# w_down's operands over other buffers of w_up, two sums of w_up in the preparation tiles, and the second half's first left parts behind the result copies

## The chip, the cores and the metric

The kernel runs on one core of one Trainium2 chip. A core has a matmul engine (TensorE, PE in the profile, with its weight loads as PEld), three engines for elementwise work (VectorE or DVE, ScalarE or ACT, GpSimd or POOL), a queue that issues most of the DMAs (SyncE, SP), an on-chip memory for tiles and eight banks in which matmuls accumulate. Each engine works through its own instructions in their order and waits on semaphores for the others. The metric is the device time of one execution in microseconds.

## What is computed

One encoder layer on 2048 tokens of width 1024, in float32: a norm, one wide product, a windowed and a neighbourhood attention, gates, a projection, and then the part that matters here, the feed-forward block:

```python
x = x + merged @ w_out[l]
h2 = rms_norm(x, norm_mlp[l])
x = x + jnp.square(jax.nn.relu(h2 @ w_up[l])) @ w_down[l]      # 1024 -> 4096 -> 1024
return rms_norm(x, norm_final)
```

## The kernel before

All products in float32 are made of three matmuls: each operand is split into a rounded half (a cast on ACT, line 277) and the rest (a subtraction on DVE, line 278), and lines 281, 282 and 283 multiply high by high, high by low and low by high. A left operand (the weights in w_up, the activations in w_down) is loaded into PE, a right one streams through it. A matmul of 128 x 128 by 128 x 512 is the unit.

**w_up** multiplies in two halves of the tokens (m = 0, 1), each in eight quads (q) of the 4096 features. A quad is one step of a seven-product scheme (Strassen's, in Winograd's form): products n = 1, 5, 6, 2, 7, 4, 3, each for two blocks a of 128 features, 12 matmuls a block, 24 a product, 168 a quad. Six of the eight banks serve a quad: x for n = 1 and 2, y for 6, 7 and 4, z for 5 and 3. What leaves a bank:

- n = 1: ACT copies x into a tile c1 (line 1497), and only then may n = 2 go on in x.
- n = 6: DVE adds y and c1 into u2, and only then may n = 7 go on in y.
- n = 2: relu and square on ACT give the block c11. n = 7, 4, 3: more sums on DVE (line 272), relu (1457) and square (1460) on ACT.
- After n = 3, DVE makes four more sums of the finished blocks (s1, a21, s2, s4), the left operands of w_down. All seven are stored to DRAM (`keep`, line 1479; tensor `at`), with tiles from the ring `c`, 11 tiles.

The left parts of a quad come from `up_left_steps`: the quad's weights lie in two tiles `uraw`, sums of them in `uS`, the seven split operands in the rings `uwhla` (one buffer) and `uwhlb` (two buffers), taken in turn. A cast into one of the three buffers has to wait for the product that read it three parts earlier. The right parts of a half lie in seven pairs of pages, `ubh1` to `ubh7`. The ring `chunk`, four tiles, serves for preparing the second half's right parts during the first half's quads 1 to 6 (`ahead`, `parts_ahead`) and is idle otherwise.

**w_down** is again one step of the seven-product scheme, now over the whole matrix. For each product n and each of 16 slices k it loads the stored block into `da` (512 KB) and the weights into `dw` (256 KB), splits them into `dah` and `dwh` (four buffers each), and runs 24 matmuls, three for each of eight banks (t = 0 to 7). The buffers of w_down are laid into the memory that w_up leaves, in the order in which the rings are made; a first write to such a buffer waits for the last reader of what lay there. Before, `dah` lies over `ubh1` and `uwhlb`, and `dwh` over `uwhla` and a part of `uraw`.

What sets the order: the program is written as a sequence, and a scheduler with its own model of times orders each engine's instructions. Marks such as `issue_after(x)` keep an instruction from being placed ahead of x; they make no wait on the chip.

Of the kernel before, what the change touches and what calls it, by code (L numbers as in the profile page):

```python
# [8 lines left out]
F32 = mybir.dt.float32  # L9
F32R = mybir.dt.float32r  # L10
# [12 lines left out]
P = 128  # L23
KC = D // P
NB = 4
BT = 512
# [66 lines left out]
def encoder_layer(ctx, tc, x, norm_mix, w_in, b_gate, sink, rpb, w_pa, w_pb, w_out,  # L93
                  norm_mlp, w_up, w_down, norm_final, dist_a, mask_b, out):
    nc = tc.nc
    V, A, G, PE, SY = nc.vector, nc.scalar, nc.gpsimd, nc.tensor, nc.sync

    def pool(name, side=None, space=None, stack=None):
        kw = {"reuse_waits": "tile"} if space is not DRAM else {}
        if side:  # L100
            kw["side"] = side
        if space:
            kw["space"] = space
        return (stack or ctx).enter_context(tc.tile_pool(name=name, bufs=1, **kw))
# [19 lines left out]
    def T(pl, shape, dt, tag, bufs):  # L124
        n_t[0] += 1
        pl = pl[tag] if isinstance(pl, dict) else pl
        return pl.tile(shape, dt, tag=tag, bufs=bufs, name=f"{tag}_{n_t[0]}")
# [131 lines left out]
    def by_token(c):  # L259

        return c.rearrange("p (t a c) -> p t a c", t=4, a=4)

    def by_place(c):

        return c.rearrange("p (a t c) -> p t a c", t=4, a=4)
# [10 lines left out]
    def split(src, hi, lo, eng):  # L276
        rounded[0] = A.copy(hi, src).ins  # L277
        return eng.tensor_tensor(out=lo, in0=src, in1=hi.bitcast(F32), op=ALU.subtract).ins  # L278
# [10 lines left out]
    def ring(stack, tag, shape, dt, bufs, side="right"):  # L289

        pl = pool(f"r_{tag}", side=side, stack=stack)
        return lambda: T(pl, shape, dt, tag, bufs)
# [17 lines left out]
    def zbank(pl, bufs=1):  # L310
        n_ps[0] += 1
        return pl.tile([P, 512], F32, tag="b", bufs=bufs, name=f"zb_{n_ps[0]}")
# [265 lines left out]
    right = {n: (in_page[n](), in_page[n]()) for n in (1, 2)}  # L578
    tbanks = [(tpool, 2), (zpool[0], 1), (tpool, 2), (zpool[1], 1), (ypool[0], 1), (ypool[1], 1)]
    for k in range(KC):  # L580
        ps = zbank(*tbanks[k % 6])
# [21 lines left out]
    for p in range(2):  # L603
        t = T(xp, [P, D], F32, "xin", 8).rearrange("p (k c) -> p k c", k=4)
        c = QUADS[2][0]
# [14 lines left out]
    for k in range(KC):  # L620
        ps = zbank(*tbanks[k % 6])
# [135 lines left out]
    for q in range(2, len(QUADS)):  # L757
# [15 lines left out]
        if q == SECOND:  # L773
            right, b0 = right2, 2
# [5 lines left out]
        lf = list(in_left(ws, QUADS[q][1], (1, 2) if q == 2 else (), ORDER if q == 2 else ORDER_3))  # L780
# [485 lines left out]
    up_page, up_rings = {}, {}  # L1266
# [14 lines left out]
    def up_whl():  # L1281
        n_whl[0] += 1
        return (up_rings["whla"] if n_whl[0] % 3 == 1 else up_rings["whlb"])()

    def up_weights(q, behind=None):
        ws = []
        for p in range(2):
            w = up_rings["raw"]()
            with tc.issue_after(behind) if behind else nullcontext():
                SY.dma_start(w, w_up[0][p * BT : (p + 1) * BT, q * BT : (q + 1) * BT].rearrange("(k p) f -> p k f", p=P))  # L1290
            ws.append(w)
        return ws

    def up_left(ws, behind=None):

        out = {}
        for _ in up_left_steps(ws, out, behind):
            pass
        return out

    def up_left_steps(ws, out, behind=None, eng=V):

        a11, a21 = ws[0][:, :, 0:256], ws[0][:, :, 256:512]
        a12, a22 = ws[1][:, :, 0:256], ws[1][:, :, 256:512]

        def parts(src, eng):
            hl = up_whl()
            split(src, hl[:, 0], hl[:, 1], eng)
            return hl

        with tc.issue_after(behind) if behind else nullcontext():
            out[1] = parts(a11, V)
        yield
        s1 = up_rings["S"]()
        with tc.issue_after(behind) if behind else nullcontext():
            add(V, s1, a21, a22)
        out[5] = parts(s1, V)
        yield
        add(eng, a21, a11, a21, ALU.subtract)
        s2 = up_rings["S"]()  # L1320
        add(eng, s2, a22, a21, ALU.subtract)
        out[6] = parts(s2, eng)
        yield
        out[2] = parts(a12, eng)
        yield
        out[7] = parts(a21, eng)
        yield
        out[4] = parts(a22, eng)
        last_left[0] = rounded[0]
        yield  # L1330
        add(eng, a12, a12, s2, ALU.subtract)
        out[3] = parts(a12, eng)
# [134 lines left out]
            yield  # L1467
        next(rights, None)

    def up_quad(m, q, lf, right, spread):  # L1470

        x, y, z = [None] * 2, [None] * 2, [None] * 2
        c1, u2, c11, c22 = [None] * 2, [None] * 2, [None] * 2, [None] * 2

        def plus(out, ps, c):
            return add(V, by_token(out), by_place(ps), by_token(c))

        def keep(n, a, c):
            stored[0] = SY.dma_start(ats[n][2 * q + a][:, m], c).ins

        for n in (1, 5, 6, 2, 7, 4, 3):
            hl, (rh, rl) = lf[n], right[n]
            last = None
            for a in range(2):
                if n == 1:
                    x[a] = bank()
                elif n == 5:
                    z[a] = bank()
                elif n == 6:
                    y[a] = bank()  # L1490
                ps = {1: x, 2: x, 5: z, 3: z, 6: y, 7: y, 4: y}[n][a]
                at = slice(a * P, (a + 1) * P)
                for k in range(4):
                    mm3s(ps, hl[:, 0, k, at], hl[:, 1, k, at], rh[:, k], rl[:, k], k == 0 and n in (1, 5, 6), k == 3)
                if n == 1:
                    c1[a] = up_rings["c"]()
                    A.copy(by_token(c1[a]), by_place(ps))  # L1497
                elif n == 6:
                    u2[a] = up_rings["c"]()
                    last = plus(u2[a], ps, c1[a])  # L1500
                elif n == 2:
                    c11[a] = up_rings["c"]()
                    squared(c11[a], ps)
                    keep(1, a, c11[a])
                elif n == 7:
                    c22[a] = up_rings["c"]()
                    plus(c22[a], ps, c1[a])
                    last = plus(c22[a], z[a], c22[a])
                    squared(c22[a])
                    keep(4, a, c22[a])  # L1510
                elif n == 4:
                    last = plus(c1[a], ps, c1[a])
                    squared(c1[a])
                    keep(2, a, c1[a])
                elif n == 3:
                    a11, a12, a21, a22 = c11[a], c1[a], u2[a], c22[a]
                    last = plus(a21, ps, a21)
                    squared(a21)
                    s1, s2, s4 = up_rings["c"](), up_rings["c"](), up_rings["c"]()
                    add(V, s1, a21, a22)  # L1520
                    keep(5, a, s1)
                    add(V, a21, a11, a21, ALU.subtract)
                    keep(7, a, a21)
                    add(V, s2, s1, a11, ALU.subtract)
                    keep(6, a, s2)
                    add(V, s4, a12, s2, ALU.subtract)
                    keep(3, a, s4)
            if last:
                with tc.issue_after(last):
                    next(spread, None)  # L1530
# [176 lines left out]
    rights, lf, rest = started  # L1707
    for _ in range(2):
        right = next(rights)
# [7 lines left out]
    for m in range(2):  # L1717
        if m:
            right = next(rights)
            lf = up_left(up_weights(0))  # L1720
        next(rights, None)
        ws = None
        for q in range(8):
            lf = up_left(ws, page_done[0] if m == 0 and q == 1 else None) if q else lf
            if m == 0 and q == 6:
                rights = up_right(1)
                next(rights)
            spread = last_page(rights) if m == 0 and q == 0 else iter(())
            if m == 0 and 1 <= q < 7:
                spread = ahead(q - 2) if 2 <= q < 6 else parts_ahead(1 if q == 1 else 5)  # L1730
            next(spread, None)
            if q < 7:
                ws = up_weights(q + 1, last_dma[0] if m == 0 and q == 0 else None)
            up_quad(m, q, lf, right, spread)
    s_up.close()


    s_dn = ctx.enter_context(ExitStack())
    dw = ring(s_dn, "dw", [P, BT], F32, 8)
    da = ring(s_dn, "da", [P, 2, BT], F32, 4)  # L1740
    dwh = ring(s_dn, "dwh", [P, 2, BT], F32R, 4)
    dah = ring(s_dn, "dah", [P, 2, 2, BT], F32R, 4)
    dt = ring(s_dn, "dt", [P, BT], F32, 2)
    t2_ = ring(s_dn, "t2", [P, BT], F32, 16)
    x2_ = ring(s_dn, "x2", [P, BT], F32, 8)
    p5_ = ring(s_dn, "p5", [P, BT], F32, 8)
    junk_ = ring(s_dn, "junk", [P, BT], F32, 2)
# [20 lines left out]
    t2 = [None] * 16  # L1768
# [89 lines left out]
    for n in (1, 6, 2, 7, 5, 3, 4):  # L1858
        for group in ((range(8),) if n != 4 else (range(4), range(4, 8))):
# [9 lines left out]
            for k in range(16):  # L1869
                lf, rt = left(n, k, part), right_(n, k)  # L1870
# [52 lines left out]
```

## Time and profile before

| | |
|---|---|
| three runs | 2592.23, 2597.12, 2599.40 us (median 2597.12) |
| the profiled execution | 2594.54 us, span of its instructions 2592.8 us |
| w_up, first half | about 1387 to 1666 us of the span |
| w_up, second half | about 1666 to 1972 us |
| w_down | about 1974 us to the end |
| granted matmul clock, mean | 0.997 |

All times in the rows are us from the span's start, each from one profiled execution. A timeline row has the start, the duration, engine, source line, operation, output and inputs with their buffer numbers left out, a count of merged instructions, and in brackets how long the engine had been idle before and what ended it. A row of grouped instructions has busy us and mean ns of one behind the bar. A row of windows has, after the stretch, its length and the busy time of PE, PEld, DVE, ACT and POOL, each with a count, then the granted clock, the DMA engines' busy share and GB/s. A row of the waits has engine and line that waited, whom for, the total in us, how often, and the longest.

### The profile page before, as it was taken

How to read it: one execution, taken by the hardware profiler on the slowest of the kernel's cores; microseconds unless marked ns; L12 is line 12 of the kernel's file. 1: busy time of each engine (PE TensorE's matmuls, PEld its weight loads, DVE VectorE, ACT ScalarE, POOL GpSimd, SP SyncE). 2: the span in 40 equal slices, each digit the busy share in tenths (PEclk: the TensorE clock that was granted, in tenths of full speed). 3: DMA queues.
4: the chain of work that ended last, by engine and by line, in shares of the span. 5: the costliest groups of instructions: out<-in, count | busy, mean ns of one | idle time of the engine just before them, and what ended most of it. 6: DMA issues, size and time to landing. Idle time of an engine off the chain costs nothing.

```text
span 2592.8 us, 34576 instructions
## 1 busy us (share of the span) xinstructions
PE 2541.9 (98%) x11936; PEld 2115.2 (82%) x11936; DVE 1695.4 (65%) x2693; ACT 1311.0 (51%) x2345; POOL 411.9 (16%) x506
## 2 busy tenths in 40 slices
PE   7999999999999999999999999999999999999998
PEld 6788888887887988888887888888887888888887
DVE  8866676667674577646597767866665535554766
ACT  6365464556775676524356555644444322323444
POOL 1000101133345765130312000000000000000011
PEclk9999999999999999999999999999999999999999
DMA  5768868774457899688888666744438835444564
GB/s 187 219 197 249 286 219 275 238 226 112 112 140 190 215 292 264 212 302 304 299 314 257 230 210 224 272 168 164 148 112 297 295 102 186 143 155 157 185 202 162
DMA packets 347999, 552.39 MB, mean 213 GB/s; under 512 B 32120, under 2 KB 152424, under 8 KB 345776
## 3 DMA queue, kind: packets, MB, share of 16 engines
q1 hardware_dynamic: 330640, 509.66, 61.7%
q10 hardware_dynamic: 10944, 24.12, 2.5%
q0 software_dynamic: 6240, 16.40, 2.1%
q8 instruction: 94, 1.54, 0.2%
q14 instruction: 81, 0.66, 0.1%
HBM read 363.35 MB, written 186.71 MB: 212 GB/s over the span
## 4 chain that ended last, share of the span: by engine, by line
PE 84%; DMA 5%; DVE 5%; ACT 2%; issue 1%; SPq 1%; POOL 0%; POOLq 0%; DVEq 0%; ACTq 0%
PE b L282 16%; PE b L283 16%; PE b L281 16%; PE zb L283 5%; PE zb L281 5%; PE zb L282 5%; PE mm L202 3%; PE mm L204 3%; PE mm L203 3%; PE av L1137 2%; PE pt L1157 2%; PE s L1111 1%; PE pt L893 1%; PE b L202 1%; PE b L204 1%
## 5 line engine op out<-in xcount | busy, mean ns | idle before, releaser
L282 PE MATMUL b<-dwh,dah 128*128 128x512 f32 x896 | 348.7, 389 | 0.4 <-DVE dwh L278 0.4
L283 PE MATMUL b<-dwh,dah 128*128 128x512 f32 x896 | 347.7, 389 | 0.0
L281 PE MATMUL b<-dwh,dah 128*128 128x512 f32 x896 | 338.5, 389 | 1.7 <-ACT dwh L277 1.7
L277 ACT CAST dah<-da 128x1024 fp32r<-128x1024 f32 (+1 forms) x128 | 120.8, 946 | 368.6 <-PE b L283 245.8
L281 PE MATMUL zb<-zh,zwhl 128*128 128x512 f32 x728 | 284.6, 391 | 4.0 <-ACT zc L488 1.4
L282 PE MATMUL zb<-zh,zwhl 128*128 128x512 f32 x728 | 284.6, 391 | 0.0
L283 PE MATMUL zb<-zh,zwhl 128*128 128x512 f32 x728 | 283.4, 391 | 1.2 <-DVE zwhl L278 1.2
L278 DVE TENSOR_TENSOR dah<-da,dah 128x1024 fp32r<-128x1024 f32 (+1 forms) x128 | 139.3, 1090 | 213.0 <-ACT dah L277 209.9
L282 PE MATMUL b<-ubh,uwhlb 128*128 128x512 f32 x592 | 231.5, 391 | 3.7 <-DVE ubh L278 3.7
L281 PE MATMUL b<-ubh,uwhlb 128*128 128x512 f32 x592 | 230.7, 390 | 2.3 <-ACT uc L1497 1.6
L283 PE MATMUL b<-ubh,uwhlb 128*128 128x512 f32 x592 | 229.8, 390 | 0.0
L281 PEld LDWEIGHTS b<-dwh,dah 128*128 128x128 f32 x896 | 168.1, 188 | 37.0 <-ACT dwh L277 2.1
L282 PEld LDWEIGHTS b<-dwh,dah 128*128 128x128 f32 x896 | 168.2, 188 | 35.7 <-DVE dwh L278 0.8
L283 PEld LDWEIGHTS b<-dwh,dah 128*128 128x128 f32 x896 | 168.2, 188 | 34.9
L272 DVE TENSOR_TENSOR uc<-b,uc 128x512 f32<-128x512 f32 x160 | 108.9, 689 | 112.8 <-PE b L283 106.9
L281 PEld LDWEIGHTS zb<-zh,zwhl 128*128 128x128 f32 x728 | 136.8, 188 | 34.3 <-ACT zc L488 2.5
L283 PEld LDWEIGHTS zb<-zh,zwhl 128*128 128x128 f32 x728 | 136.7, 188 | 30.0 <-DVE zwhl L278 2.2
L282 PEld LDWEIGHTS zb<-zh,zwhl 128*128 128x128 f32 x728 | 136.7, 188 | 27.9
L202 PE MATMUL mm<-zh,whl 128*128 128x512 f32 x368 | 154.6, 420 | 1.7 <-DVE z L1015 0.9
L204 PE MATMUL mm<-zh,whl 128*128 128x512 f32 x368 | 144.7, 393 | 0.0
L203 PE MATMUL mm<-zh,whl 128*128 128x512 f32 x368 | 144.4, 392 | 0.0
L282 PEld LDWEIGHTS b<-ubh,uwhlb 128*128 128x128 f32 x592 | 111.5, 188 | 27.8 <-DVE ubh L278 4.8
(268 smaller groups left out, 5726.8 us busy)
## 6 DMA issues: line engine op xcount, KB each, us to landing
at<-uc SPq DMA_DIRECT2D x224, 256.0 KB, 2.0
da<-at SPq DMA_DIRECT2D x96, 512.0 KB, 5.0
dw<-in_w_down_dram SPq DMA_DIRECT2D x160, 256.0 KB, 3.7
uraw<-in_w_up_dram SPq DMA_DIRECT2D x32, 1024.0 KB, 13.2
pgl<-wo_d SPq DMA_DIRECT2D x28, 1024.0 KB, 6.3
zraw<-in_w_in_dram SPq DMA_DIRECT2D x24, 1024.0 KB
z<-zg SPq DMA_DIRECT2D x64, 256.0 KB, 5.4
qs_a<-ze SPq DMA_DIRECT2D x32, 256.0 KB, 5.8
```

What stands on the lines that cost most here:

```text
L202: PE.matmul(ps, lh, rh, start=first, stop=False)
L203: PE.matmul(ps, lh, rl, start=False, stop=False)
L204: PE.matmul(ps, ll, rh, start=False, stop=last)
L272: return eng.tensor_tensor(out=out, in0=a, in1=b, op=op).ins
L277: rounded[0] = A.copy(hi, src).ins
L278: return eng.tensor_tensor(out=lo, in0=src, in1=hi.bitcast(F32), op=ALU.subtract).ins
L281: PE.matmul(ps, lh, rh, start=first, stop=False, skip_group_check=True)
L282: PE.matmul(ps, lh, rl, start=False, stop=False, skip_group_check=True)
L283: PE.matmul(ps, ll, rh, start=False, stop=last, skip_group_check=True)
L893: last = PE.transpose(pt[:, h * P : (h + 1) * P], s[:, h, c * P : (c + 1) * P], ident).ins
L1137: PE.matmul(po[0][:, i0 * P : (i0 + ni) * P], v[:kp, c, :], src[:kp, o : o + ni * P], start=first[0], stop=(c == 7 and z == 1), skip_group ...
L1157: last = PE.transpose(pt[:kp, at + (i - i0) * P : at + (i - i0 + 1) * P], s[i][:, rr : rr + kp], ident)
```

## The change

There are three edits. First, the rings of w_down are made in another order: `t2` comes before `dah`, and `dah` before `dwh`. `dah` now lies over `ubh5` and `ubh1`, `dwh` over `ubh6` and `uS`, and `t2` over the buffers of the left parts. Second, in the second half of w_up (and in quad 7 of the first), s1 and s2 take their tiles from `chunk` instead of `c`. Third, at the start of the second half only three of the seven left parts of quad 0 are written ahead of the quad; the four others stand in the quad behind the copies of n = 1.

```diff
-    def up_quad(m, q, lf, right, spread):
+    def up_quad(m, q, lf, right, spread, rest=()):
...
                 if n == 1:
                     c1[a] = up_rings["c"]()
-                    A.copy(by_token(c1[a]), by_place(ps))
+                    copied = A.copy(by_token(c1[a]), by_place(ps)).ins
...
-                    s1, s2, s4 = up_rings["c"](), up_rings["c"](), up_rings["c"]()
+                    of = "chunk" if m or q == 7 else "c"
+                    s1, s2, s4 = up_rings[of](), up_rings[of](), up_rings["c"]()
...
+            for _ in range(5 if rest and n == 1 else 0):
+                with tc.issue_after(copied):
+                    next(rest, None)
...
         if m:
             right = next(rights)
-            lf = up_left(up_weights(0))
+            lf = {}
+            rest = up_left_steps(up_weights(0), lf)
+            for _ in range(3):
+                next(rest)
...
-            up_quad(m, q, lf, right, spread)
+            up_quad(m, q, lf, right, spread, rest if m == 1 and q == 0 else ())
...
+    t2_ = ring(s_dn, "t2", [P, BT], F32, 16)
+    dah = ring(s_dn, "dah", [P, 2, 2, BT], F32R, 4)
     dwh = ring(s_dn, "dwh", [P, 2, BT], F32R, 4)
-    dah = ring(s_dn, "dah", [P, 2, 2, BT], F32R, 4)
     dt = ring(s_dn, "dt", [P, BT], F32, 2)
-    t2_ = ring(s_dn, "t2", [P, BT], F32, 16)
```

The number of instructions on each engine stays the same. Up to the last quad of the first half no engine's order changes.

ACT at the start of w_up's second half. `uwhla` and `uwhlb` are the left parts of quad 0, here those of n = 2, 7 and 4; the two COPY rows are n = 1's copies. Before:

```order
L1460 ACTIVATE uc_15778<-uc_15778 128x512
L277 CAST uwhlb_15981<-uraw_15965 128x1024
L1460 ACTIVATE uc_15793<-uc_15793 128x512
L277 CAST uwhla_15984<-uraw_15963 128x1024
L277 CAST uwhlb_15987<-uraw_15965 128x1024
L1497 COPY uc_16051<-b_16038 128x512
L1497 COPY uc_16066<-b_16053 128x512
L1459 ACTIVATE uc_16136<-b_16038 128x512
```

After the change:

```order
L1460 ACTIVATE uc_15778<-uc_15778 128x512
L1460 ACTIVATE uc_15793<-uc_15793 128x512
L1497 COPY uc_16038<-b_16025 128x512
L1497 COPY uc_16053<-b_16040 128x512
L277 CAST uwhlb_16055<-uraw_15965 128x1024
L277 CAST uwhla_16058<-uraw_15963 128x1024
L277 CAST uwhlb_16061<-uraw_15965 128x1024
L1459 ACTIVATE uc_16136<-b_16025 128x512
```

The two copies stand ahead of the three casts; before, they stood behind them.

DVE at the same place, after the change. `b_16094` and `b_16109` are the two banks of n = 6; the L278 rows are the second halves of the left parts of n = 2, 7 and 4:

```order
L272 TENSOR_TENSOR uchunk_15937<-uchunk_15936,uc_15823 128x512
L272 TENSOR_TENSOR uc_15938<-uc_15737,uchunk_15937 128x512
L272 TENSOR_TENSOR uc_16107<-b_16094,uc_16038 128x512
L272 TENSOR_TENSOR uc_16122<-b_16109,uc_16053 128x512
L278 TENSOR_TENSOR uwhlb_16055<-uraw_15965,uwhlb_16055 128x1024
L278 TENSOR_TENSOR uwhla_16058<-uraw_15963,uwhla_16058 128x1024
L272 TENSOR_TENSOR uraw_15965<-uraw_15965,uS_15976 128x4x256
L278 TENSOR_TENSOR uwhlb_16061<-uraw_15965,uwhlb_16061 128x1024
L272 TENSOR_TENSOR uS_16285<-uraw_16023,uraw_16021 128x1024
```

Before, these three L278 rows, the uraw difference and the uS stood among the sums of quad 7, ahead of the two sums that empty n = 6. PE takes n = 2 (banks `b_16025`, `b_16040`) and the beginning of n = 7 so, after the change:

```order
L283 MATMUL b_16109<-ubh_1843_15957,uwhlb_15978 128x512
L281 MATMUL b_16025<-ubh_1853_15987,uwhlb_16055 128x512
L282 MATMUL b_16025<-ubh_1854_15988,uwhlb_16055 128x512
L281 MATMUL b_16040<-ubh_1853_15987,uwhlb_16055 128x512
L282 MATMUL b_16040<-ubh_1854_15988,uwhlb_16055 128x512
L281 MATMUL b_16094<-ubh_1856_15995,uwhla_16058 128x512
L282 MATMUL b_16094<-ubh_1857_15996,uwhla_16058 128x512
L281 MATMUL b_16109<-ubh_1856_15995,uwhla_16058 128x512
L282 MATMUL b_16109<-ubh_1857_15996,uwhla_16058 128x512
L283 MATMUL b_16025<-ubh_1853_15987,uwhlb_16055 128x512
```

Eight matmuls that need only the cast halves come ahead of the first that needs a DVE half (the last row); before, L281, L282 and L283 of n = 2 alternated from its start.

ACT at the start of w_down. `uc` rows are the last quad of w_up, `dah` and `dwh` the first slices k = 0 to 3. Before:

```order
L1460 ACTIVATE uc_17930<-uc_17930 128x512
L277 CAST dah_18258<-da_18257 128x1024
L277 CAST dah_18292<-da_18291 128x1024
L277 CAST dah_18326<-da_18325 128x1024
L277 CAST dah_18360<-da_18359 128x1024
L1457 ACTIVATE uc_17945<-uc_17945 128x512
L1457 ACTIVATE uc_17986<-uc_17986 128x512
L277 CAST dwh_18262<-dw_18263 128x512
L277 CAST dwh_18296<-dw_18297 128x512
```

After the change:

```order
L277 CAST dah_18258<-da_18257 128x1024
L277 CAST dwh_18262<-dw_18263 128x512
L1457 ACTIVATE uc_18065<-uc_18065 128x512
L1460 ACTIVATE uc_18065<-uc_18065 128x512
L277 CAST dah_18292<-da_18291 128x1024
L277 CAST dwh_18296<-dw_18297 128x512
L1457 ACTIVATE uc_17930<-uc_17930 128x512
L277 CAST dah_18326<-da_18325 128x1024
L1460 ACTIVATE uc_17930<-uc_17930 128x512
L277 CAST dwh_18330<-dw_18331 128x512
L277 CAST dah_18360<-da_18359 128x1024
L277 CAST dwh_18364<-dw_18365 128x512
```

The pairs of a slice stand together, and begin ahead of relu and square of two blocks. DVE follows in the same manner, after the change (`b_17988` is the second bank of y, `b_17947` and `b_17960` are the banks of z):

```order
L278 TENSOR_TENSOR dah_18258<-da_18257,dah_18258 128x1024
L278 TENSOR_TENSOR dwh_18262<-dw_18263,dwh_18262 128x512
L272 TENSOR_TENSOR uc_17930<-b_17973,uc_17930 128x512
L278 TENSOR_TENSOR dah_18292<-da_18291,dah_18292 128x1024
L278 TENSOR_TENSOR dwh_18296<-dw_18297,dwh_18296 128x512
L278 TENSOR_TENSOR dah_18326<-da_18325,dah_18326 128x1024
L278 TENSOR_TENSOR dwh_18330<-dw_18331,dwh_18330 128x512
L272 TENSOR_TENSOR uc_17945<-b_17988,uc_17945 128x512
L272 TENSOR_TENSOR uc_17986<-b_17947,uc_17986 128x512
L278 TENSOR_TENSOR dah_18360<-da_18359,dah_18360 128x1024
L278 TENSOR_TENSOR dwh_18364<-dw_18365,dwh_18364 128x512
L272 TENSOR_TENSOR uc_18001<-b_17960,uc_18001 128x512
```

The sums that empty the last banks now stand between the splits of the pairs; before, three of these four stood ahead of all of them and the last one behind the first two. On PE, the first product of w_down takes L281, L282 and L283 of a bank together; before, the eight L281 of slice 0 came first. The bank after `b_17947` is written by its 15th matmul, the one after `b_17960` by its 26th.

## The prediction

> **What bounds the kernel now.** I read the page's first part, then the table of waits for the matmul engine from 1390 us to the end, then two stages.
>
> ```profile
> PE 2541.9 (98%) x11936; PEld 2115.2 (82%) x11936; DVE 1695.4 (65%) x2693; ACT 1311.0 (51%) x2345; POOL 411.9 (16%) x506
> ...
> PE b L281 <- ACT dwh L277: 1.7, 1, 1.7
> PE b L281 <- ACT uc L1497: 1.6, 1, 1.6
> PE b L282 <- DVE dwh L278: 0.4, 1, 0.4
> ...
> 1700.00:1956.00 256.00, 256.00 (x1131) 211.99 (x1130) 162.32 (x193) 117.28 (x165) 0.00 (x0) 1.00 0.38 134
> 1990.00:2580.00 590.00, 590.00 (x2604) 488.55 (x2603) 334.85 (x462) 211.81 (x328) 10.88 (x12) 1.00 0.55 183
> ```
>
> The matmul engine (PE) sets the end: 98% of the span. In the part that the change reaches, it waits three times, 3.7 us in all: at the start of w_up's second half (L1497) and at the start of w_down (the two dwh rows). Between and behind these places it never pauses; 256.00 us for 1131 matmuls is 0.2263 us each. So what the other engines gain or lose there is worth nothing unless it reaches PE.
>
> **First place: the start of w_up's second half.** PE's and ScalarE's (ACT's) timelines:
>
> ```profile
> 1681.92 0.39 PE L283 MATMUL b<-ubh,uwhlb 128*128 128x512 f32 x1
> 1683.93 0.50 PE L281 MATMUL b<-ubh,uwhlb 128*128 128x512 f32 x1 [1.62 <-ACT uc L1497]
> 1684.27 0.40 PE L282 MATMUL b<-ubh,uwhlb 128*128 128x512 f32 x1
> ...
> 1674.74 0.64 ACT L1460 ACTIVATE uc<-uc 128x512 f32<-128x512 f32 x1
> 1676.91 1.06 ACT L277 CAST uwhla<-uraw 128x1024 fp32r<-128x1024 f32 x1 [1.53 <-PE b L283]
> 1682.35 1.04 ACT L277 CAST uwhlb<-uraw 128x1024 fp32r<-128x1024 f32 x1 [4.38 <-PE b L283]
> 1683.30 1.07 ACT L1497 COPY uc<-b 128x512 f32<-128x512 f32 x2
> ```
>
> The copies could go from 1675 on, but stand behind a cast that waits for PE's sixth product (n=6) to give its buffer back. PE's next matmul was due at 1681.92 + 0.23 = 1682.15, came at 1683.93, and the one after it 0.34 instead of 0.23 later: 1.78 + 0.11 = 1.89 us lost.
>
> In the new order the copies follow the square that began at 1674.74. The second also needs VectorE's (DVE's) first sum to have read its buffer, below at about 1676.1. Both are done by 1677, five us before PE wants their banks: this wait is gone. What is late next? The second halves of three left parts now stand on DVE behind the two sums that empty n=6.
>
> ```profile
> 1674.37 1.23 DVE L272 TENSOR_TENSOR uS<-uraw,uraw 128x1024 f32<-128x1024 f32 x1
> 1675.50 0.69 DVE L272 TENSOR_TENSOR uc<-uc,uc 128x512 f32<-128x512 f32 x1
> 1676.10 1.23 DVE L278 TENSOR_TENSOR uwhlb<-uraw,uwhlb 128x1024 fp32r<-128x1024 f32 x1
> 1677.24 1.23 DVE L272 TENSOR_TENSOR uraw<-uraw 128x1024 f32<-128x1024 f32 x1
> ...
> 1687.26 1.28 DVE L272 TENSOR_TENSOR uc<-b,uc 128x512 f32<-128x512 f32 x2
> ```
>
> DVE ran without a pause from 1674.37 to 1687.26. Five 1.23 us operations leave this stretch (three left halves, an uraw difference, a uS); each holds DVE for 1.14 (1677.24 less 1676.10 is the step to the next), so its sums end at 1687.26 - 5.7 = 1681.6. The first emptying sum follows at once; the second needs the end of n=6, which released ACT at 1682.35, and with 0.69 is done at 1683.04. The left half of n=2 then ends at 1683.0 + 1.23 = 1684.2. PE has eight matmuls that don't need it: 1682.15 + 8 x 0.2263 = 1683.96. It waits 0.25 and restarts 0.11 late: 0.36 lost. The later parts have more room (n=7's half by 1685.3, due at 1684.2 + 20 x 0.2263 = 1688.7). **Gain 1.89 - 0.36 = 1.5 us**; bounds 0.8 (DVE a further 0.7 us late) and 1.9.
>
> The sums in the preparation tiles (the chunk ring) remove waits for stores from the c ring; the list of PE's waits has none for that, so alone they are worth nothing. The next quad writes these four tiles again 38 us later (168 matmuls x 0.2263), when their 256 KB stores are long out. One DMA moves:
>
> ```profile
> 1681.97 0.38 SPq L1290 DMA_DIRECT2D uraw<-in_w_up_dram  x1
> 1704.28 1.22 DVE L278 TENSOR_TENSOR uwhlb<-uS,uwhlb 128x1024 fp32r<-128x1024 f32 x1
> ...
> uraw<-in_w_up_dram SPq DMA_DIRECT2D x32, 1024.0 KB, 13.2
> ```
>
> A weight load for quad 2 now waits on SyncE's queue (SP) for n=7's left half, so it is issued at 1685.3 instead of 1681.97, and the stores of n=2 behind it with it. With 13.2 us it lands at 1698.5; DVE wants it behind the row of 1704.28. Three us late costs nothing; without these 6 us of cover a late load would hold DVE, and PE only after that.
>
> **Second place: the start of w_down.**
>
> ```profile
> 1972.16 0.39 PE L283 MATMUL b<-ubh,uwhla 128*128 128x512 f32 x1
> 1974.20 2.14 PE L281 MATMUL b<-dwh,dah 128*128 128x512 f32 x8 [1.65 <-ACT dwh L277]
> 1976.72 0.50 PE L282 MATMUL b<-dwh,dah 128*128 128x512 f32 x1 [0.39 <-DVE dwh L278]
> 1977.06 0.39 PE L283 MATMUL b<-dwh,dah 128*128 128x512 f32 x1
> ...
> 1966.35 1.04 ACT L277 CAST dah<-da 128x1024 fp32r<-128x1024 f32 x1
> 1969.64 2.96 ACT L277 CAST dah<-da 128x1024 fp32r<-128x1024 f32 x3 [2.25 <-PE b L283]
> 1973.54 2.17 ACT L277 CAST dwh<-dw 128x512 fp32r<-128x512 f32 x4
> ...
> 1963.29 6.97 DMA dw<-in_w_down_dram
> ```
>
> The second dah cast waited 2.25 us for PE to finish with the buffer below it, and the first dwh cast for PE's last matmul of w_up. PE's next matmul was due at 1972.39; the ninth, due 8 x 0.2263 later at 1974.20, came at 1976.72. 2.52 + 0.11 = 2.63 us are lost.
>
> With operands over buffers whose last reader is quad 7's n=1, 5 or 6, no cast of the first four pairs waits for PE, and the pairs follow each other: dah, dwh, dah, dwh. The first pair had landed by 1966.35 (da) and by 1970.26 at the very latest (the chain's last dw load, 1963.29 + 6.97).
>
> ```profile
> L272 DVE TENSOR_TENSOR uc<-b,uc 128x512 f32<-128x512 f32 x80 | 54.4, 690 | 70.5 <-PE b L283 69.9
> L278 DVE TENSOR_TENSOR dah<-da,dah 128x1024 fp32r<-128x1024 f32 x6 | 7.1, 1219 | 0.6 <-ACT dah L277 0.6
> L278 DVE TENSOR_TENSOR dwh<-dw,dwh 128x512 fp32r<-128x512 f32 x6 | 3.9, 685 | 0.0
> L277 ACT CAST dah<-da 128x1024 fp32r<-128x1024 f32 x6 | 6.1, 1051 | 9.0 <-PE b L283 9.0
> L277 ACT CAST dwh<-dw 128x512 fp32r<-128x512 f32 x6 | 3.4, 612 | 0.0
> ```
>
> First pair: 1966.35 + 1.05 + 0.61 + 1.22 + 0.69 = 1969.9, before 1972.39. What is behind the new work on DVE: the sums that empty w_up's last banks. The z bank's first one stands behind the third pair. Had that pair landed only at 1970.26, 1.05 + 0.64 (a square) + 0.61 + 0.69 + 2 x 0.69 makes 1974.6; PE reads that bank with its 15th matmul, 1972.39 + 14 x 0.2263 = 1975.56. The last emptying sum, behind the fourth pair, is done by 1974.6 + 1.22 + 0.69 + 0.69 = 1977.2, wanted by the 26th matmul at 1978.05. Both hold by 0.9 us at worst. **Gain 2.6 us**; lower bound 0.8, if the first product still waits for a dwh (2.63 - 1.78).
>
> **Sum.** 1.5 + 2.6 = 4.1 us off the profiled execution's 2594.54 (1.7 of it outside the span): 2590.4. Nothing before 1670 moves. The four times known of the kernel before (three runs, one profiled) average 2595.8, 1.3 above the profiled one, so I expect 2591.7, which is 5.4 under the median 2597.12 (0.21%).
>
> **A rule on the clock.** The rows behind the two waits:
>
> ```profile
> 1684.00:1690.00 6.00, 6.00 (x27) 4.96 (x28) 4.51 (x7) 1.90 (x4) 0.00 (x0) 1.00 0.99 349
> 1974.00:1977.00 3.00, 2.42 (x9) 1.71 (x10) 3.00 (x4) 3.00 (x7) 0.00 (x0) 1.00 0.99 313
> ```
>
> The granted clock is 1.00 behind both, so no slow matmuls are in my sum. The Trainium skill, "TensorE: Matmul & The Clock Gate" (HAM oscillation), says that a PE pause of over some 3.4 us puts the array back to half clock until it has been busy as long again; by it 1.6 us pauses are too short, as the trace agrees, and two longer ones would, as an estimate from that page, have cost 1.7 us each on top.
>
> **Rivals.**
> - Only one place gains: DVE lags in the first (say the weights for uS land late), or the first pair in the second. For: DVE holds only 0.7 us of reserve at the first. Against: its chain there is known row by row. 1.5 or 2.6 gained: 2594.3 or 2593.2.
> - The runs' excess over the profile sits in these two waits. They differ by 7.2 us; if the pauses lengthen with late loads, all runs come down to the same 2590.4, 6.7 under the median. For: both places see DMA near 1.0. Against: nothing shows where the excess lies.
> - Slower: the emptying sums on DVE stand behind loads. If the third pair lands late, the two z banks stay full and PE stops inside the first w_down product, us for us. From 0.9 us (by the bound above) it eats the gain, from 0.9 + 4.1 = 5.0 us late the kernel is slower; 14 us late gives 2595.8 + 9 = 2605. For: the queue is full (1.0 there). Against: the first eight loads are issued in the same order behind the same waits.
> - The change doesn't do what it says: the first pair's loads, not the buffers, hold the start; the first place alone then counts, or nothing: 2595.8.
>
> **How the numbers follow.** Forecast 60%, only one place 13%, the runs' excess 17%, slower 6%, nothing 4%. The median of three runs scatters by some 3 us (7.2 between three). Within 0.3% (7.8 us, about what a measurement of this kernel can tell from no change) lie most of the forecast (52 of 60), half of the excess case (9), 12 of 13 and 3 of 4, and 1 of the slow case: 77%. Faster by more: 8 + 8 = 16%, from scatter on a true 4 to 7 us. Slower: 7%. The range goes from 2587 (4.5 us, the whole loss, and a low run) to 2599 (nothing gained and a high run).
>
> **What would show it.** Right: no PE wait on L1497's copy, and at most some 0.3 us on a uwhlb half near 1684; the first w_down matmul 0.23 us behind the last of w_up, both halves of its first pair done before it; about 4 us less span, and 0.2263 us a matmul elsewhere. Wrong: a PE wait over 0.5 us for DVE's uc sums or for dah/dwh in the first 6 us of w_down, a new wait anywhere from 1700 to 1956 or beyond 1990, or a span that falls by less than 2 us or more than 6.

## The result: 0.17% less, and both waits gone

| | before | after |
|---|---|---|
| median (22 runs each) | 2597.11 us | 2593.01 us |
| lowest to highest | 2592.23 to 2603.46 | 2589.18 to 2600.08 |
| ratio after / before | | 0.9983, 95% interval 0.9976 to 0.9991 |
| profiled execution / its span | 2594.54 / 2592.8 us | 2592.82 / 2591.0 us |

The forecast was 2591.7 us in a range of 2587 to 2599, with no change beyond 0.3% as the likeliest class. The ratio is worth 4.1 us off the median (2597.11 - 2593.01), with an interval of 2.3 to 6.2 us. Two executions far off the others, of 6596.85 us (one of the eleven of e1) and 14324.78 us (one of the fifteen of before beside e5), are left out of the ratios below.

PE's waits in the changed kernel, from the last quad of w_up's first half to the end (engine and line that waited, whom for, total us, times, longest):

```profile
core 0 of [0], span 2591.0 us
engine line waited for: us in total, times, longest us
PE b L283 <- DVE uwhlb L278: 0.2, 1, 0.2
```

Of the three waits of before in this part (1.7, 1.6 and 0.4 us) none is left, and one short one is new: the one for DVE's half of n = 2's left part that the prediction named. PE's timeline of the changed kernel at the first place (start, duration, idle time ahead and its end in brackets):

```profile
1673.63 0.39 PE L281 MATMUL b<-ubh,uwhla 128*128 128x512 f32 x1
...
1684.28 0.39 PE L283 MATMUL b<-ubh,uwhlb 128*128 128x512 f32 x1
1684.51 0.39 PE L281 MATMUL b<-ubh,uwhlb 128*128 128x512 f32 x1
...
1686.10 0.39 PE L282 MATMUL b<-ubh,uwhla 128*128 128x512 f32 x1
1686.65 0.50 PE L283 MATMUL b<-ubh,uwhlb 128*128 128x512 f32 x1 [0.17 <-DVE uwhlb L278]
1686.99 0.39 PE L281 MATMUL b<-ubh,uwhlb 128*128 128x512 f32 x1
```

n = 2 begins 0.23 us behind n = 6 (1684.28 to 1684.51). The ninth matmul was due at 1686.10 + 0.23 = 1686.33, came at 1686.65, and the next one is 0.34 behind it: 0.32 + 0.11 = 0.43 us lost, where the kernel before lost 1.89. ACT and DVE there, after the change:

```profile
1676.93 0.57 ACT L1497 COPY uc<-b 128x512 f32<-128x512 f32 x1
1678.87 0.59 ACT L1497 COPY uc<-b 128x512 f32<-128x512 f32 x1 [1.36 <-issue]
...
1684.71 1.06 ACT L277 CAST uwhlb<-uraw 128x1024 fp32r<-128x1024 f32 x1 [3.35 <-PE b L283]
```
```profile
1683.57 0.69 DVE L272 TENSOR_TENSOR uc<-uc,uchunk 128x512 f32<-128x512 f32 x1
1684.18 1.28 DVE L272 TENSOR_TENSOR uc<-b,uc 128x512 f32<-128x512 f32 x2
1685.38 1.21 DVE L278 TENSOR_TENSOR uwhlb<-uraw,uwhlb 128x1024 fp32r<-128x1024 f32 x1
```

The copies are done by 1679.5, five us ahead of PE's need; the cast that used to stand ahead of them still waits for the end of n = 6 and holds nobody up. The second place, PE and then DVE:

```profile
1973.07 0.39 PE L283 MATMUL b<-ubh,uwhla 128*128 128x512 f32 x1
1973.30 0.39 PE L281 MATMUL b<-dwh,dah 128*128 128x512 f32 x1
```
```profile
1966.14 0.69 DVE L278 TENSOR_TENSOR dwh<-dw,dwh 128x512 fp32r<-128x512 f32 x1
...
1971.45 1.28 DVE L272 TENSOR_TENSOR uc<-b,uc 128x512 f32<-128x512 f32 x2
...
1974.38 0.68 DVE L272 TENSOR_TENSOR uc<-b,uc 128x512 f32<-128x512 f32 x1
```

w_down follows w_up without a pause. Its first pair was complete at 1966.83, 6.5 us early; the last emptying sums end at 1972.73 and 1975.06, 3.7 and 3.9 us ahead of the 15th and 26th matmul (1973.30 + 14 and 25 x 0.2263).

**Why the span fell by only 1.8 us.** The first row of PE's timeline above (1673.63) is PE's first matmul of n = 5 in the second half's quad 0; no order had changed for PE ahead of it. In the kernel before it stands here:

```profile
1671.27 0.39 PE L281 MATMUL b<-ubh,uwhla 128*128 128x512 f32 x1
```

So this execution of the changed kernel was 2.36 us late (1673.63 - 1671.27) before the change had acted on PE. The spans are given to 0.1 us only, so the distance from that mark to the end is taken from a row of windows, whose length stands behind the stretch. Before, and then after the change:

```profile
1671.27:2592.77 921.50, 909.56 (x4009) 751.83 (x4007) 549.49 (x725) 368.28 (x555) 14.65 (x17) 1.00 0.53 178
1673.63:2591.02 917.39, 908.94 (x4009) 752.46 (x4007) 548.79 (x726) 368.00 (x555) 14.61 (x17) 1.00 0.53 179
```

It is 917.39 us after the change and 921.50 before: 4.11 us less. All experiments below are read by this distance.

### The profile page after: what moved, and what is told of

Same layout as the page of the kernel before. It is cut to its first block, busy times and chain, and to the rows that moved or that the text cites. A ratio compares the mean times of both kernels' runs of the same rounds, so it can differ in the third digit from the quotient of the medians.

```text
span 2591.0 us, 34565 instructions
## 1 busy us (share of the span) xinstructions
PE 2539.7 (98%) x11936; PEld 2115.5 (82%) x11936; DVE 1696.5 (65%) x2693; ACT 1309.7 (51%) x2345; POOL 409.5 (16%) x506
## 4 chain that ended last, share of the span: by engine, by line
PE 83%; DMA 6%; DVE 5%; ACT 2%; issue 2%; SPq 1%; POOL 0%; DVEq 0%; POOLq 0%; ACTq 0%
PE b L283 17%; PE b L282 17%; PE b L281 17%; PE zb L281 4%; PE zb L283 4%; PE zb L282 4%; PE mm L202 3%; PE mm L204 3%; PE mm L203 3%; PE av L1137 2%; PE pt L1157 2%; PE s L1111 1%; PE pt L893 1%; PE b L203 1%; PE b L204 1%
## 5 line engine op out<-in xcount | busy, mean ns | idle before, releaser
L282 PE MATMUL b<-dwh,dah 128*128 128x512 f32 x896 | 348.9, 389 | 0.0
L283 PE MATMUL b<-dwh,dah 128*128 128x512 f32 x896 | 348.0, 389 | 0.0
L281 PE MATMUL b<-dwh,dah 128*128 128x512 f32 x896 | 339.6, 389 | 0.0
L278 DVE TENSOR_TENSOR dah<-da,dah 128x1024 fp32r<-128x1024 f32 (+1 forms) x128 | 139.3, 1089 | 231.6 <-ACT dah L277 228.6
L281 PE MATMUL zb<-zh,zwhl 128*128 128x512 f32 x728 | 284.8, 392 | 3.9 <-ACT zc L488 1.3
L282 PE MATMUL zb<-zh,zwhl 128*128 128x512 f32 x728 | 284.9, 391 | 0.0
L283 PE MATMUL zb<-zh,zwhl 128*128 128x512 f32 x728 | 283.7, 391 | 1.2 <-DVE zwhl L278 1.2
L282 PE MATMUL b<-ubh,uwhlb 128*128 128x512 f32 x592 | 231.4, 391 | 4.6 <-DVE ubh L278 4.6
L281 PE MATMUL b<-ubh,uwhlb 128*128 128x512 f32 x592 | 231.1, 391 | 0.7 <-DVE uc L272 0.7
L283 PE MATMUL b<-ubh,uwhlb 128*128 128x512 f32 x592 | 230.2, 391 | 0.2 <-DVE uwhlb L278 0.2
L282 PEld LDWEIGHTS b<-dwh,dah 128*128 128x128 f32 x896 | 168.3, 188 | 34.8
L283 PEld LDWEIGHTS b<-dwh,dah 128*128 128x128 f32 x896 | 168.3, 188 | 34.8
L281 PEld LDWEIGHTS b<-dwh,dah 128*128 128x128 f32 x896 | 168.3, 188 | 34.8
L281 PEld LDWEIGHTS zb<-zh,zwhl 128*128 128x128 f32 x728 | 136.8, 188 | 34.8 <-ACT zc L488 2.5
L283 PEld LDWEIGHTS zb<-zh,zwhl 128*128 128x128 f32 x728 | 136.8, 188 | 29.7 <-DVE zwhl L278 2.0
L282 PEld LDWEIGHTS zb<-zh,zwhl 128*128 128x128 f32 x728 | 136.8, 188 | 27.8
L282 PEld LDWEIGHTS b<-ubh,uwhlb 128*128 128x128 f32 x592 | 111.6, 189 | 28.6 <-DVE ubh L278 5.4
```

Source lines behind the costliest of these rows:

```text
L281: PE.matmul(ps, lh, rh, start=first, stop=False, skip_group_check=True)
L282: PE.matmul(ps, lh, rl, start=False, stop=False, skip_group_check=True)
L283: PE.matmul(ps, ll, rh, start=False, stop=last, skip_group_check=True)
```

## The experiments

The profiled executions, cut at the mark, at the last matmul of w_up and at the first of w_down (us):

| kernel | mark at | mark to last of w_up | to first of w_down | from there to the end | mark to end |
|---|---|---|---|---|---|
| before | 1671.27 | 300.89 | 2.04 | 618.57 | 921.50 |
| after | 1673.63 | 299.44 | 0.23 | 617.72 | 917.39 |
| e1: rings alone | 1675.56 | 300.89 | 0.23 | 617.73 | 918.85 |
| e2: left parts and chunk, old rings | 1674.67 | 299.43 | 2.03 | 618.57 | 920.03 |
| e3: after without chunk | 1676.37 | 299.44 | 0.22 | 617.74 | 917.40 |
| e4: chunk alone | 1674.75 | 300.89 | 2.04 | 618.57 | 921.50 |
| e5: four left parts ahead | 1675.66 | 298.97 | 0.23 | 617.73 | 916.93 |
| e6: late sums, 5 | 1672.16 | 299.47 | 0.23 | 621.98 | 921.68 |
| e7: late sums, 12 | 1674.18 | 299.43 | 0.23 | 628.98 | 928.64 |

**e1, the rings alone.** The kernel before with

```diff
+    t2_ = ring(s_dn, "t2", [P, BT], F32, 16)
+    dah = ring(s_dn, "dah", [P, 2, 2, BT], F32R, 4)
     dwh = ring(s_dn, "dwh", [P, 2, BT], F32R, 4)
-    dah = ring(s_dn, "dah", [P, 2, 2, BT], F32R, 4)
     dt = ring(s_dn, "dt", [P, BT], F32, 2)
-    t2_ = ring(s_dn, "t2", [P, BT], F32, 16)
```

> The kernel before with w_down's rings in the new order alone. Theory (two separate waits, each worth its own loss): at the start of w_up's second half PE still waits about 1.6 us for L1497's copy; at the start of w_down no PE wait for dah or dwh is left, and the first w_down matmul comes 0.23 us behind the last of w_up. From PE's first matmul of n=6 in the second half's quad 0 to the end of the span: 2.6 us shorter than before; time 2.6 us (0.10%) less, ratio 0.9990 within its scatter. Rival (only the first place gains): a PE wait of 1.5 to 2.5 us for a dah or dwh stays, time unchanged. Rival (the emptying sums stand behind late loads): a new PE wait for DVE's uc sums in the first 6 us of w_down.

Measured, PE's waits from 1660 us to the end:

```profile
core 0 of [0], span 2594.4 us
engine line waited for: us in total, times, longest us
PE b L281 <- ACT uc L1497: 1.6, 1, 1.6
```

The waits of w_down's start are gone, the copy's is untouched, and from the mark to the end it is 2.65 us less than before (921.50 - 918.85; expected 2.6). No emptying sum holds PE. The time cannot show it: 0.9998 of before, interval 0.9987 to 1.0009, which includes both 0.9990 and 1. This execution reached the mark 4.3 us later than that of before.

**e2, the left parts behind the copies, with the chunk sums.** The change without its edit to the rings; against the changed kernel:

```diff
     s_dn = ctx.enter_context(ExitStack())
...
-    t2_ = ring(s_dn, "t2", [P, BT], F32, 16)
-    dah = ring(s_dn, "dah", [P, 2, 2, BT], F32R, 4)
     dwh = ring(s_dn, "dwh", [P, 2, BT], F32R, 4)
+    dah = ring(s_dn, "dah", [P, 2, 2, BT], F32R, 4)
     dt = ring(s_dn, "dt", [P, BT], F32, 2)
+    t2_ = ring(s_dn, "t2", [P, BT], F32, 16)
```

> The kernel before with the left parts of the second half behind the copies, and the two sums in the chunk tiles; w_down's rings in the old order. Theory: no PE wait for L1497's copy; one short wait of about 0.2 us for DVE's half of uwhlb near the ninth matmul of n=2 (0.4 us lost with the restart); the two dwh waits of 1.7 and 0.4 us at the start of w_down stay. From n=6 to the end of the span 1.5 us shorter than before; time 1.5 us less, ratio 0.9994 within its scatter. Rival (only w_down's start gains): the copy's wait stays in another form, time unchanged.

Measured, the same view:

```profile
core 0 of [0], span 2594.7 us
engine line waited for: us in total, times, longest us
PE b L281 <- ACT dwh L277: 1.7, 1, 1.7
PE b L282 <- DVE dwh L278: 0.4, 1, 0.4
PE b L283 <- DVE uwhlb L278: 0.2, 1, 0.2
```

1.47 us less than before (921.50 - 920.03; expected 1.5); time 0.9991 of before, interval 0.9979 to 1.0004, which includes 1, too. The two parts add up: 2.65 + 1.47 = 4.12, and the whole change has 4.11. They are two separate waits; the rival that only one of them gains falls.

**e3, the change without the chunk sums.** Against the changed kernel:

```diff
-                    of = "chunk" if m or q == 7 else "c"
-                    s1, s2, s4 = up_rings[of](), up_rings[of](), up_rings["c"]()
+                    s1, s2, s4 = up_rings["c"](), up_rings["c"](), up_rings["c"]()
```

> The changed kernel with the two sums s1 and s2 back in tiles of the ring c. Theory of the prediction (the chunk sums are worth nothing): the waits and the time of the changed kernel, no PE wait but the 0.2 us one. Rival (the copies now go so early that the ring c has no free tile; the chunk sums make it): the first copy must wait until DVE has read the tile it takes over, and the second for the store of a21, which leaves about 1680.6 in the changed kernel's trace and takes some 2.9 us, so about 1683.5; behind the copies stands the cast for n=2, which then ends at about 1685.1 where PE wants it at 1684.5. So a new PE wait of 0.5 to 1.5 us on the cast of uwhlb or on L1497, and from n=6 to the end of the span 0.3 to 1.3 us longer than the changed kernel.

Measured, ACT's timeline at the first place:

```profile
1677.67 1.66 ACT L1460 ACTIVATE uc<-uc 128x512 f32<-128x512 f32 x3
1684.24 1.32 ACT L1497 COPY uc<-b 128x512 f32<-128x512 f32 x2 [4.91 <-DVE uc L272]
1685.45 1.06 ACT L277 CAST uwhlb<-uraw 128x1024 fp32r<-128x1024 f32 x1
```

The rival's mechanism is there: without the chunk tiles the copies wait 4.91 us for the ring c, and the cast for n = 2 stands behind them. It ends at 1686.51, and PE, whose mark is 2.74 us later in this execution than in the changed kernel's, wants it at 1684.51 + 2.74 = 1687.25. 0.7 us of cover are left, so the rival's price is nought: PE's only wait is the 0.2 us one, and from the mark to the end it is 917.40, 0.01 more than the changed kernel. Time 0.9992 of before, interval 0.9981 to 1.0002: it cannot be told from before nor from the changed kernel (0.9983). My expectation of a wait took the store of a21 as slower than it was: I had put 2.9 us from issue to landing, and stores took 2.0 to 3.4 us there, the one that released the second copy 2.0.

**e4, the chunk sums alone.** The kernel before with the first two lines of e3's diff in place of the third.

> The kernel before with the two sums in the chunk tiles alone. Theory: nothing (the copies stand behind the cast for n=4, which waits for the end of n=6 in any case): PE waits of 1.6 us for the copy and of 1.7 and 0.4 us for dwh as before, time within the scatter of before, ratio 1.000. Rival (stores hold something up that the list of waits does not show): some of PE's waits shorter, up to 1.5 us less.

Measured: the three waits of 1.7, 1.6 and 0.4 us, 921.50 us from the mark to the end (before 921.50), time 1.0004 of before, interval 0.9994 to 1.0014. Nothing, as forecast. It serves as a second profile of the old waits, too: two executions whose marks are 3.5 us apart agree to 0.01 us behind it.

**e5, a version without the last wait.** The change with

```diff
-            for _ in range(5 if rest and n == 1 else 0):
+            for _ in range(4 if rest and n == 1 else 0):
...
-            for _ in range(3):
+            for _ in range(4):
                 next(rest)
```

> The changed kernel, but with four left parts of the second half's quad 0 ahead of it (n = 1, 5, 6 and 2) and only n = 7, 4 and 3 behind the copies. Theory: the wait of 0.2 us for DVE's half of uwhlb goes, since that half now stands among the sums of quad 7; the copies still stand ahead of the cast for n=4, so no wait for them. DVE has 3.4 us more ahead of the two sums that empty n=6 (the half, an uraw difference and a uS), so these end near 1688.9 in the changed kernel's trace, 1.0 us before n=7 wants its banks at 1684.51 + 24 x 0.2263 = 1689.94, and the half of n=7 is done near 1690.1, 0.5 us before its first matmul. From n=5 of that quad to the end of the span 0.44 us less than the changed kernel's 917.37: 916.9. Rival (what is put ahead only moves the wait): a wait of 0.2 to 1 us for DVE at the start of n=7, 917.3 or more. The time itself: 0.2% less than before, not to be told from the changed kernel.

Measured: from 1660 us to the end PE waits for nothing at all. DVE, and PE's first matmul of n = 7:

```profile
1680.34 1.22 DVE L278 TENSOR_TENSOR uwhlb<-uraw,uwhlb 128x1024 fp32r<-128x1024 f32 x1
...
1689.10 1.28 DVE L272 TENSOR_TENSOR uc<-b,uc 128x512 f32<-128x512 f32 x2
1690.30 1.21 DVE L278 TENSOR_TENSOR uwhla<-uraw,uwhla 128x1024 fp32r<-128x1024 f32 x1
```
```profile
1691.98 0.39 PE L281 MATMUL b<-ubh,uwhla 128*128 128x512 f32 x1
```

The half of n = 2 is early, the sums that empty n = 6 end at 1690.38, 1.6 us before n = 7 begins, and the half of n = 7 is ready at 1691.51. From the mark to the end it is 916.93 us, as expected, 4.57 less than before and 0.46 less than the changed kernel. Time: median 2592.44 us, 0.9980 of before, interval 0.9970 to 0.9990. It beats the kernel before; from the changed kernel (0.9983) the times do not tell it apart, the profile does.

**e6 and e7, the emptying sums made late.** The changed kernel, with further sums ahead of a z bank's last one (they write the tile of s1, which the sum s1 writes again behind them; the tiles of s1, s2 and s4 are taken ahead of them), and PE's matmuls of w_down's first slices held to the plain order of the banks. Both ran once. The main lines of e6; e7 has 12 in place of 5:

```diff
...
+                    for _ in range(5 if m and q == 7 and a == 0 else 0):
+                        plus(s1, ps, a21)
                     last = plus(a21, ps, a21)
...
-                mm3s(banks[t], lf[:, 0, t // 4, at], lf[:, 1, t // 4, at], rt[:, 0], rt[:, 1], k == 0, k == 15)
+                with tc.issue_after(before_[0]) if n == 1 and k < 3 and before_[0] else nullcontext():
+                    before_[0] = mm3s(banks[t], lf[:, 0, t // 4, at], lf[:, 1, t // 4, at], rt[:, 0], rt[:, 1], k == 0, k == 15)
```

> The changed kernel with a late emptying sum: on the way out of w_up, the first z bank's sum is preceded by five more sums on DVE into a tile that is written again later, and PE takes the eight banks of w_down's first product in plain order. With the dah and dwh splits that fall in between, the sum starts at 1977.4 instead of 1972.05 in the changed kernel's trace, 5.3 us later, and ends at 1978.1. PE wants that bank with its 13th matmul of w_down, 1973.30 + 12 x 0.2263 = 1976.0. Theory by the trace of the changed kernel (reserve 3.3 us here): PE waits 2.0 us and loses 2.1 with the restart, from n=5 to the end of the span 919.5. Rival (the prediction's worst-case reserve of 0.9 us, 0.45 here): a wait of 4.9 us. Rival (the banks do not set PE's start): no wait, 917.4. The clock: after a wait of 2 us every matmul 0.2263 us.

> The same with twelve more sums: the bank's sum ends 5.5 us later than with five, at about 1983.6 (seven sums of 0.6 us and two of the weights' sums between them). Theory: PE waits 7.6 us, loses 7.7 with the restart, 925.1 from n=5 to the end of the span if the clock stays; if a pause of that length brings the half clock that the kernel before shows behind its pauses near 1384 (eight matmuls of 0.43 us in place of 0.2263), 1.6 us more, 926.7. Rival (banks do not set PE's start): 917.4.

Measured for e6, PE, DVE, and the granted clock behind the pause (eighth column of the window: 0.57):

```profile
1974.35 0.39 PE L283 MATMUL b<-dwh,dah 128*128 128x512 f32 x1
1977.09 0.47 PE L281 MATMUL b<-dwh,dah 128*128 128x512 f32 x1 [2.35 <-DVE uc L272]
...
1978.33 0.59 PE L283 MATMUL b<-dwh,dah 128*128 128x512 f32 x1
1978.71 0.63 PE L281 MATMUL b<-dwh,dah 128*128 128x512 f32 x1
1979.14 0.63 PE L282 MATMUL b<-dwh,dah 128*128 128x512 f32 x1
...
1981.97 0.40 PE L283 MATMUL b<-dwh,dah 128*128 128x512 f32 x1
```
```profile
1974.09 2.13 DVE L272 TENSOR_TENSOR uchunk<-b,uc 128x512 f32<-128x512 f32 x3
1976.26 0.69 DVE L272 TENSOR_TENSOR uc<-b,uc 128x512 f32<-128x512 f32 x1
```
```profile
1978.00:1982.00 4.00, 4.00 (x13) 3.09 (x12) 3.99 (x8) 0.76 (x2) 0.00 (x0) 0.57 1.05 407
```

The bank's sum does hold PE: it ends at 1976.95, PE goes on at 1977.09, due at 1974.58, so 2.51 us late (expected 2.0). The first of the five further sums began at 1970.56, where the bank's own would have stood; made 5.70 us late it cost 2.51, so the reserve in this order is 3.2 us (expected 3.3; the worst-case bound would have left 0.45). But 921.68 from the mark to the end is 4.29 more than the changed kernel, not 2.1. The rest is nearly all the clock: from 1978.33 to about 1981.8 a matmul takes 0.43 us. From 1977.09 to 1981.97 there are 14 steps in 4.88 us, 1.71 more than 14 x 0.2263; 0.08 of that is the restart (0.31 us to the second matmul). My expectation that the clock stays after 2 us was wrong.

e7, PE and the clock:

```profile
1985.56 0.77 PE L281 MATMUL b<-dwh,dah 128*128 128x512 f32 x1 [8.84 <-DVE uc L272]
1986.12 0.63 PE L282 MATMUL b<-dwh,dah 128*128 128x512 f32 x1
...
1990.28 0.39 PE L283 MATMUL b<-dwh,dah 128*128 128x512 f32 x1
```
```profile
1986.00:1990.00 4.00, 4.00 (x11) 3.03 (x11) 3.19 (x6) 0.71 (x2) 0.00 (x0) 0.50 0.45 166
```

PE is 9.0 us late (due at 1976.56; expected 7.6) and loses 2.2 more to the clock (11 steps in 4.72 us): 928.64, or 11.25 above the changed kernel. The pause was longer than planned because each further sum cost 0.72 us instead of 0.60 (below).

## Why the prediction was right, step by step

- **First place, 1.89 us lost before, 0.36 after, gain 1.5.** Right in each part. Less the 2.36 us of the mark, the copies were done at 1677.1 (forecast by 1677), DVE's older sums at 1681.8 (1681.6) and n = 2's half at 1684.2 (1684.2). The loss is 0.43 instead of 0.36, since PE resumed 0.06 us after DVE's end. e2 shows the gain alone: 1.47.
- **The chunk sums, nothing.** Right alone (e4) and within the change (e3). Its reason was incomplete: they do remove a wait of 4.9 us, ACT's and not PE's, which the new place of the copies would otherwise bring, and which 0.7 us of slack still hides.
- **The late weight load, nothing.** It was issued at 1687.76, or 1685.4 less the 2.36 (forecast 1685.3), and PE has no wait for what it feeds.
- **Second place, gain 2.6.** e1 shows it alone: 2.65. Its lower bound, 0.8, took off 1.78 us, which is the delay of the first place; PE's delay at this one is 1974.20 - 1972.39 = 1.81, and the bound stays 0.8. The reserve of the emptying sums was put at 0.9 us at worst; in the changed kernel it is 3.7 and 3.9, since the first pairs landed earlier than the bound allowed.
- **The sum, 4.1 us.** 4.11 in the trace, 4.1 in the medians. The forecast time was 1.3 us too low because its base was: I took 2595.8, the mean of the four times then known, and the median of before is now 2597.11. That is the one term of the sum that was mis-sized.
- **A test of mine that fails.** "A span that falls by less than 2 us" was to show the prediction wrong. The two spans differ by 1.8 us, and still the gain is 4.11: the executions differ by 2.36 us ahead of the change. The test should have been put on the distance from the last place that both kernels share.
- **The rivals.** One place alone: falls (e1, e2). The runs' excess in the waits: falls. Marks lie from 1671.27 to 1676.37 us, 5.1 us apart, while kernels with the same waits agree within 0.01 us behind them; and the runs of the changed kernel scatter as widely as before (10.9 and 11.2 us). Slower by emptying sums: the mechanism is real (e6, e7), the reserve is four times what I allowed, and past it the price was steeper than "us for us" in both executions, by some 1.6 and 2.2 us of half clock. The change not doing what it says: falls.
- **The clock.** In this kernel the removed pauses cost no clock, as said: behind them matmuls ran on at 0.23 us in before, e1, e2 and e4. But the rule from the Trainium skill ("TensorE: Matmul & The Clock Gate", HAM oscillation) gave no safe margin: the removed waits of 1.62 and 1.65 us lie close below the 1.85 us of idle time in one window of the clock that halved it (last section).

Not settled: where in the first 1670 us the 5 us of scatter arise in full. The start of w_up is one place (below).

## What to carry to other kernels

A gain of a few us in a kernel whose runs scatter by ten is read from one profile of each kernel, as the distance from the last instruction that both share to the end: here it repeats to 0.01 us, where ten runs beside 35 of before could not tell 2.7 us from nothing. Neither wait at the border of two stages was here for late data: one came from a buffer laid over one that is read last, the other from an early copy queued behind a cast that had to wait. What has to be checked is who stands behind the instruction that moved, with how many us of slack. Slack that ran out was not paid us for us once PE stood idle for more than about half of one 3.41 us window of its clock.

## What the runs showed of the hardware

**Half clock follows a 3.41 us window in which PE stood idle for about half; no pause of 3.4 us is needed.** The Trainium skill, "TensorE: Matmul & The Clock Gate" (HAM oscillation), puts the array back to half clock behind a pause of over some 3.4 us. The measurement differs: e6 shows half clock behind 2.35 us idle. Its cost agrees: I had estimated 1.7 us from that page, and e6 measures 1.71 with the restart, 1.63 without.

In the nine traces the granted clock changes only at times that lie whole multiples of 3.413 us apart. In e6 half clock begins at 814.41, 923.64, 1377.61 and 1978.35 us, the last three 32, 165 and 341 times 3.413 us behind the first. Up to the last 10 us of the span it lasts one such window each time, or two or three. So what counts is how much of one window PE stands idle. Three pairs of windows, from e6, from e4 and from the changed kernel; the first of each pair holds PE's pauses, the second lies behind it:

```profile
1974.94:1978.35 3.41, 1.26 (x6) 1.07 (x7) 2.67 (x5) 1.82 (x3) 0.00 (x0) 1.00 1.04 408
1978.36:1981.76 3.40, 3.40 (x10) 2.62 (x9) 3.40 (x6) 0.25 (x1) 0.00 (x0) 0.50 1.03 401
...
1388.20:1391.61 3.41, 1.56 (x6) 1.05 (x7) 3.38 (x4) 2.29 (x4) 0.00 (x0) 1.00 1.01 371
1391.62:1395.02 3.40, 3.40 (x10) 2.63 (x9) 1.84 (x4) 3.38 (x6) 0.00 (x0) 0.50 1.02 357
...
1388.60:1392.01 3.41, 2.06 (x8) 1.46 (x9) 2.93 (x3) 1.89 (x4) 0.00 (x0) 1.00 1.00 362
1392.01:1395.42 3.41, 3.41 (x17) 2.80 (x16) 1.92 (x3) 3.30 (x6) 0.00 (x0) 1.00 1.01 363
```

PE is idle for 3.41 - 1.26 = 2.15 us in the first of these windows, and for 1.85 and 1.35 in the two others; the clock behind them is 0.50, 0.50 and 1.00. The last two executions have nearly the same pauses at the start of w_up, 0.7 and 1.35 us with one matmul between; in e4 most of both falls into one window, in the changed kernel only the second does. From 1366 to 2570 us, all nine profiles together have eleven windows at full clock with 1.85 us idle or more, and half clock follows each of them. They have eleven with 1.35 to 1.65 us idle, and it follows none; the removed waits are six of these. So the boundary here lies between 1.65 and 1.85 us, about half a window. It also depends on where a window's edge falls: e1's pause of 1.87 us at 1428.77, cut by an edge into 0.43 and 1.44 us, left the clock as it was. The place of the windows is not tied to the kernel, as the Trainium skill has it, too ("TensorE: Matmul & The Clock Gate", What's actually happening). In the stages before 1366 us, which also have shorter matmuls, the boundary is less sharp: windows with 1.46 to 1.92 us idle went either way.

**Sums that each wait for the one before cost more.** In e7 six sums into the same tile, each waiting for the one before it, took 4.30 us; less the last one's 0.68 that is 0.72 from start to start, where independent sums of the same size start 0.60 apart (two in 1.28 us).

```profile
1976.54 4.30 DVE L272 TENSOR_TENSOR uchunk<-b,uc 128x512 f32<-128x512 f32 x6
```
